# A row maximum on one core: GpSimd takes 128-column parts of rows in place of full rows, the last two rows come in chained halves, and loads are written ahead

## The chip, the cores and the metric

One core of a Trainium2 chip. The metric is the device time of one execution in microseconds (us), the slowest core's; with one core there is just that one. Most executions of a kernel agree within 0.2%.

## The reference

```python
x: float32 [32, 512, 1024]          # standard normal draws, 67.1 MB
def reference(x):
    return np.max(x, axis=-1).astype(np.float32)     # [32, 512]
```

That is 16384 rows of 1024 numbers. They are laid on 128 partitions, 128 rows on each. In this document "a row" is one such step: 1024 columns on all 128 partitions, 0.524 MB.

## The kernel before

VectorE takes the maximum of nearly all rows directly from a ring of 46 rows in SBUF. Five rows are taken from it: TensorE transposes the row (`turn`), ScalarE copies it out of PSUM, GpSimd takes the maximum over the partitions, and TensorE transposes one partition of the result back (`back`) into a small PSUM tile, which the traces call `fetched`; below this last step is the *fetch*. A tiny reduction of VectorE, the merge, ends it. The last row comes in two halves, and the result of the first half is stored in the column just ahead of the second, so that the second reduction (513 columns) takes it in. Loads are counted from 0, and step j is the stretch of the program that reduces load j.

```python
BLOCKS = [[15, 15, 15, 13, 13, 11, 9, 9, 6, 6],      # rows in each load
          [3, 3, 2, 1, 1, 1, 1, 1, 1, 1]]
RING = 46
TENSOR = {8: [("turn", 8, 0), ("back", 8, 0)],  # what TensorE does, by the step ahead of which it is written
          9: [("turn", 9, 0), ("turn", 9, 1), ("turn", 9, 2), ("back", 9, 0)],
          12: [("turn", 12, 0), ("back", 9, 1), ("back", 9, 2), ("back", 12, 0)]}
BY_GPSIMD = {8: 1, 9: 3, 12: 1}                 # load: full rows
MERGE = {9: 8, 15: 9, 18: 12}                   # after step: merge of load
...
        for n in loads:
            ...
            nc.sync.dma_start(out=xc, in_=xb[:, b:b + n, :])
            ...
            m = BY_GPSIMD.get(j, 0)
            ...
            for what, i, k in TENSOR.get(j, []):
                (turn if what == "turn" else back)(i, k)
            reduce = in_turn("DVE", nc.vector.reduce_max(
                out=cols[:, :n - m], in_=xc[:, :n - m, :], axis=X))
            if j in MERGE:
                i = MERGE[j]
                in_turn("DVE", nc.vector.reduce_max(out=tiles[i][1], in_=backs[i], axis=X))
...
    nc.sync.dma_start(out=half, in_=xb[:, b, :H])
    nc.sync.dma_start(out=tail[:, PAD:], in_=xb[:, b, H:])
    in_turn("DVE", nc.vector.reduce_max(out=tail[:, PAD - 1:PAD], in_=half, axis=X))
    in_turn("DVE", nc.vector.reduce_max(out=res[:, I - 1:], in_=tail[:, PAD - 1:], axis=X))
```

`in_turn` keeps the instructions of an engine in the order in which the program writes them. The waits between engines are not written by hand: they are derived from which instructions touch the same memory.

## Time and profile before

| | before |
|---|---|
| time, median of 3 runs | 164.49 us (164.41 to 164.53) |
| span of the profiled run | 162.6 us |
| load queue, share of 16 DMA engines | 96.6% |
| VectorE busy | 135.0 us (83%), of which 0.5 us in merges |
| GpSimd busy | 16.3 us, five maxima of 3.2 us |
| end of VectorE's last reduction | 160.36 us |

The load queue is the bound: by the packet records the DMA engines are full from 1.7 us to about 158.4 us. VectorE's reductions wait 24.3 us, all of it for loads. This line is of the waits of the kernel before (who waited for whom; us in total, times, longest). In the profile DVE is VectorE, PE TensorE, ACT ScalarE, POOL GpSimd and SP the engine that issues the loads; L139 is line 139 of that run's kernel:

```profile
DVE res L139 <- DMA ring<-in_x_dram: 24.3, 4, 18.9
```

There is no line in which a reduction of VectorE waits for TensorE.

### The profile page before, as it was taken

How to read it: one execution, taken by the hardware profiler on the slowest of the kernel's cores; microseconds unless marked ns; L12 is line 12 of the kernel's file. 1: busy time of each engine (PE TensorE's matmuls, PEld its weight loads, DVE VectorE, ACT ScalarE, POOL GpSimd, SP SyncE). 2: the span in 40 equal slices, each digit the busy share in tenths (PEclk: the TensorE clock that was granted, in tenths of full speed). 3: DMA queues.
4: the chain of work that ended last, by engine and by line, in shares of the span. 5: the costliest groups of instructions: out<-in, count | busy, mean ns of one | idle time of the engine just before them, and what ended most of it. 6: DMA issues, size and time to landing. Idle time of an engine off the chain costs nothing.

```text
span 162.6 us, 293 instructions
## 1 busy us (share of the span) xinstructions
PE 13.0 (8%) x80; PEld 11.7 (7%) x80; DVE 135.0 (83%) x33; ACT 6.3 (4%) x6; POOL 16.3 (10%) x9
## 2 busy tenths in 40 slices
PE   0000000000000000000000000000000040943520
PEld 0000000000000000000000000000000030933420
DVE  3000079995999779999996999999999999999994
ACT  3000000000000000000000000000000011240200
POOL 0000000000000000000000000000000007099910
PEclk9999999999999999999999999999999999985555
DMA  7999699988999799999998989999999999999990
GB/s 242 484 484 438 287 484 484 484 378 348 484 484 484 333 498 432 445 419 419 419 419 387 499 388 427 417 426 408 417 435 435 471 399 426 423 418 409 406 368 16
DMA packets 3456, 67.18 MB, mean 413 GB/s; under 512 B 640, under 2 KB 640, under 8 KB 1792
## 3 DMA queue, kind: packets, MB, share of 16 engines
q1 hardware_dynamic: 3168, 67.11, 96.6%
q10 hardware_dynamic: 288, 0.07, 0.2%
HBM read 67.11 MB, written 0.07 MB: 413 GB/s over the span
## 4 chain that ended last, share of the span: by engine, by line
DVE 54%; DMA 44%; SPq 0%; issue 0%
DVE res L139 53%; DMA ring<-in_x_dram 44%; DVE res L156 0%; DVE tail L155 0%; SPq L133 0%; DVE res L143 0%
## 5 line engine op out<-in xcount | busy, mean ns | idle before, releaser
L139 DVE TENSOR_REDUCE res<-ring 128x1 f32<-128x1024 f32 (+6 forms) x20 | 132.1, 6653 | 24.3 <-DMA ring<-in_x_dram 24.3
L106 POOL PARTITION_ALL_REDUCE top<-sb x5 | 16.1, 3255 | 138.8 <-ACT sb L104 138.8
L98 PE MATMUL ps<-ident,ring 128*128 128x128 f32 x40 | 8.1, 382 | 134.2 <-DMA ring<-in_x_dram 131.8
L98 PEld LDWEIGHTS ps<-ident,ring 128*128 128x128 f32 x40 | 7.1, 204 | 134.3 <-issue 134.2
L104 ACT COPY sb<-ps 128x1024 f32<-128x1024 f32 x5 | 5.1, 1013 | 144.9 <-PE ps L98 143.0
L115 PE MATMUL fetched<-ident,top 1*128 1x1 f32 x40 | 5.0, 243 | 9.1 <-POOL top L106 9.1
L115 PEld LDWEIGHTS fetched<-ident,top 1*128 1x128 f32 x40 | 4.6, 214 | 10.3 <-POOL top L106 9.8
L104 ACT ACT_TABLE_LOAD x1 | 1.3, 1283 | 0.7 <-PEq L176 0.7
L76 DVE MEMSET ident<- 128x128 f32 x1 | 0.2, 165 | 0.8 <-PEq L176 0.8
L156 DVE TENSOR_REDUCE res<-tail 128x1 f32<-128x513 f32 x1 | 0.7, 686 | 0.0
L155 DVE TENSOR_REDUCE tail<-ring 128x1 f32<-128x512 f32 x1 | 0.7, 675 | 0.0
L83 DVE TENSOR_SCALAR rowno<-rowno 32x1 f32<-32x1 f32 x3 | 0.4, 147 | 0.1
L143 DVE TENSOR_REDUCE res<-fetched 128x1 f32<-128x8 f32 (+1 forms) x3 | 0.5, 161 | 0.0
L78 DVE TENSOR_TENSOR_SCAN colno<-ident 128x128 f32<-128x128 f32 x1 | 0.4, 425 | 0.0
L85 DVE TENSOR_SCALAR ident<-colno,rowno 128x128 f32<-128x128 f32 x1 | 0.3, 287 | 0.0
L80 DVE STREAM_TRANSPOSE rowno<-colno 128x32 f32<-128x32 f32 x1 | 0.2, 211 | 0.0
L176 POOL MEMSET const-float32-0.0<- 128x1 f32 x1 | 0.1, 99 | 0.2 <-issue 0.2
L176 POOL MEMSET const-uint8-127<- 128x1 uint8 x1 | 0.1, 103 | 0.0
L176 POOL MEMSET const-bfloat16-1.0<- 128x1 bf16 x1 | 0.1, 102 | 0.0
L176 POOL MEMSET const-float32-1.0<- 128x1 f32 x1 | 0.1, 99 | 0.0
L77 DVE MEMSET rowno<- 128x32 f32 x1 | 0.1, 85 | 0.0
## 6 DMA issues: line engine op xcount, KB each, us to landing
ring<-in_x_dram SPq DMA_DIRECT2D x3, 7680.0 KB, 38.4
ring<-in_x_dram SPq DMA_DIRECT2D x2, 6656.0 KB, 34.6
ring<-in_x_dram SPq DMA_DIRECT2D x2, 4608.0 KB, 37.8
ring<-in_x_dram SPq DMA_DIRECT2D x2, 3072.0 KB, 31.9
ring<-in_x_dram SPq DMA_DIRECT2D x1, 5632.0 KB, 28.6
ring<-in_x_dram SPq DMA_DIRECT2D x7, 512.0 KB, 22.3
ring<-in_x_dram SPq DMA_DIRECT2D x2, 1536.0 KB, 34.9
ring<-in_x_dram SPq DMA_DIRECT2D x1, 1024.0 KB, 33.4
```

Source lines behind the costliest of these rows:

```text
L78: in_turn("DVE", nc.vector.tensor_tensor_scan(out=colno, data0=ident, data1=ident, initial=-1.0, op0=ALU.add, op1=ALU.mult))
L83: in_turn("DVE", nc.vector.tensor_scalar(out=part, in0=part, scalar1=float(q * 32), scalar2=None, op0=ALU.add))
L85: in_turn("DVE", nc.vector.tensor_scalar(out=ident, in0=colno, scalar1=rowno[:, 0:1], scalar2=None, op0=ALU.is_equal))
L98: in_turn("PE", nc.tensor.transpose(out=ps[:, c * P:(c + 1) * P], in_=rows[:, k, c * P:(c + 1) * P], identity=ident,))
L104: nc.scalar.copy(out=sb, in_=ps)
L106: nc.gpsimd.partition_all_reduce(top, sb, P, bass_isa.ReduceOp.max)
L115: in_turn("PE", nc.tensor.transpose(out=backs[j][:, k, c:c + 1], in_=tops[j, k][0:1, c * P:(c + 1) * P], identity=ident[0:1, 0:1],))
L139: reduce = in_turn("DVE", nc.vector.reduce_max(out=cols[:, :n - m], in_=xc[:, :n - m, :], axis=X))
L143: in_turn("DVE", nc.vector.reduce_max(out=tiles[i][1], in_=backs[i], axis=X))
L155: in_turn("DVE", nc.vector.reduce_max(out=tail[:, PAD - 1:PAD], in_=half, axis=X))
L156: in_turn("DVE", nc.vector.reduce_max(out=res[:, I - 1:], in_=tail[:, PAD - 1:], axis=X))
L176: nc = _bacc.Bacc("TRN2", target_bir_lowering=False, num_devices=1)
```

## The change

The intent, as the code shows it: VectorE and GpSimd share single rows. GpSimd takes the first 2 or 4 of a row's eight parts of 128 columns, so its chunks can be smaller and shared rows can come later, up to the third last row. VectorE takes the remaining columns of that row, its *part*. Loads are written into the program up to two steps ahead, so that TensorE's work, now one list, can be written as early as wanted. The last two rows come as two halves each. There are 22 transfers, as before.

```diff
 BLOCKS = [
-    [15, 15, 15, 13, 13, 11, 9, 9, 6, 6],
-    [3, 3, 2, 1, 1, 1, 1, 1, 1, 1],
+    [15, 15, 15, 8, 12, 11, 9, 8, 7, 7, 5],
+    [4, 3, 2, 2, 1, 1, 1],
 ]
 ...
+# load: (rows shared, parts of 128 columns that GpSimd takes of each)
+SHARED = {9: (5, 2), 11: (4, 2), 12: (2, 4), 14: (1, 2), 15: (1, 4), 17: (1, 2)}
+TENSOR = [
+    ("turn", 9, 0), ("turn", 9, 1), ("back", 9, 0), ("back", 9, 1),
+    ("turn", 11, 0), ("turn", 12, 0), ("back", 11, 0), ("turn", 14, 0),
+    ("turn", 15, 0), ("back", 12, 0), ("back", 14, 0), ("turn", 17, 0),
+    ("back", 15, 0), ("back", 17, 0),
+]
+MERGE = {10: (9,), 13: (11,), 16: (12,), 17: (14,), 20: (15, 17)}
 ...
+    def share(j):                 # PSUM: GpSimd's maxima and, in the last column, VectorE's
+        m, parts = SHARED[j]
+        if j not in backs:
+            fetched = psmall.tile([P, m, parts + (parts < C)], F32)
+            backs[j] = fetched
+        return backs[j]
 ...
+    for j in range(len(loads)):
+        while issued < len(loads) and issued < j + 3:
+            ...                   # stops where a ring place is still to be read
+            nc.sync.dma_start(out=rows(issued), in_=src)
+            issued += 1
+        while todo and (todo[0][0] == "back" or todo[0][1] < issued):
+            what, i, c = todo.pop(0)
+            (turn if what == "turn" else back)(i, c)
+        ...
+        if n > m:
+            maximum(res[:, col:col + n - m], rows(j)[:, :n - m, :])
+        if m and parts < C:
+            maximum(share(j)[:, :, parts], rows(j)[:, n - m:, parts * P:])
+        merge(j)
 ...
+    for t in range(2):            # the last two rows, two chained halves each
+        ...
```

More of the change, by code (lines that the diff above doesn't have):

```diff
@@ L13 @@
 BLOCKS = [
-    [15, 15, 15, 13, 13, 11, 9, 9, 6, 6],
-    [3, 3, 2, 1, 1, 1, 1, 1, 1, 1],
+    [15, 15, 15, 8, 12, 11, 9, 8, 7, 7, 5],
+    [4, 3, 2, 2, 1, 1, 1],
 ]
 RING = 46
-TENSOR = {
-    8: [("turn", 8, 0), ("back", 8, 0)],
-    9: [("turn", 9, 0), ("turn", 9, 1), ("turn", 9, 2), ("back", 9, 0)],
-    12: [("turn", 12, 0), ("back", 9, 1), ("back", 9, 2), ("back", 12, 0)],
-}
-BY_GPSIMD = {8: 1, 9: 3, 12: 1}
-MERGE = {9: 8, 15: 9, 18: 12}
+SHARED = {9: (5, 2), 11: (4, 2), 12: (2, 4), 14: (1, 2), 15: (1, 4), 17: (1, 2)}
[6 more added lines that the diff above has]
+MERGE = {10: (9,), 13: (11,), 16: (12,), 17: (14,), 20: (15, 17)}
 NOSYNC = mybir.DependencyInfo(mybir.DependencyClass.NoSync, mybir.DependencyReason.DATA)
@@ L53 @@
     allr = ctx.enter_context(tc.tile_pool(name="allr", bufs=2))
-    psum = ctx.enter_context(tc.tile_pool(name="psum", bufs=3, space=bass.MemoryType.PSUM))
-    psmall = ctx.enter_context(tc.tile_pool(name="psmall", bufs=2, space=bass.MemoryType.PSUM))
+    psum = ctx.enter_context(tc.tile_pool(name="psum", bufs=2, space=bass.MemoryType.PSUM))
+    psmall = ctx.enter_context(tc.tile_pool(name="psmall", bufs=4, space=bass.MemoryType.PSUM))
     ring = once.tile([P, RING, D], F32)
@@ L59 @@
     PAD = 16
-    tail = once.tile([P, PAD + H], F32)
+    tails = once.tile([P, 2, PAD + H], F32)
     latest = {}
@@ L86 @@
         out=ident, in0=colno, scalar1=rowno[:, 0:1], scalar2=None, op0=ALU.is_equal))
-    tiles = {}
-    tops = {}
-    backs = {}
-    def turn(j, k):
-        rows, cols = tiles[j]
-        ps = psum.tile([P, D], F32)
-        for c in range(C):
-            in_turn("PE", nc.tensor.transpose(
-                out=ps[:, c * P:(c + 1) * P],
-                in_=rows[:, k, c * P:(c + 1) * P],
-                identity=ident,
-            ))
-        sb = turned.tile([P, D], F32)
-        nc.scalar.copy(out=sb, in_=ps)
-        top = allr.tile([P, D], F32)
-        nc.gpsimd.partition_all_reduce(top, sb, P, bass_isa.ReduceOp.max)
-        tops[j, k] = top
-    def back(j, k):
-        if j not in backs:
-            fetched = psmall.tile([P, BY_GPSIMD[j], C], F32)
-            backs[j] = fetched
-        for c in range(C):
-            in_turn("PE", nc.tensor.transpose(
-                out=backs[j][:, k, c:c + 1],
-                in_=tops[j, k][0:1, c * P:(c + 1) * P],
-                identity=ident[0:1, 0:1],
-            ))
-    at = first = j = 0
+    loads = []
+    first = at = 0
     views = []
-    for loads in BLOCKS:
-        S = sum(loads) + (loads is BLOCKS[-1])
+    for sizes in BLOCKS:
+        S = sum(sizes) + 2 * (sizes is BLOCKS[-1])
         xb = xf[first * P:(first + S) * P, :].rearrange("(p i) d -> p i d", p=P)
@@ L128 @@
         b = 0
-        for n in loads:
+        for n in sizes:
             if at + n > RING:
                 at = 0
-            xc = ring[:, at:at + n, :]
-            nc.sync.dma_start(out=xc, in_=xb[:, b:b + n, :])
-            cols = res[:, first + b:first + b + n]
-            m = BY_GPSIMD.get(j, 0)
-            tiles[j] = xc[:, n - m:, :], cols[:, n - m:]
-            for what, i, k in TENSOR.get(j, []):
-                (turn if what == "turn" else back)(i, k)
-            reduce = in_turn("DVE", nc.vector.reduce_max(
-                out=cols[:, :n - m], in_=xc[:, :n - m, :], axis=X))
-            if j in MERGE:
-                i = MERGE[j]
-                in_turn("DVE", nc.vector.reduce_max(out=tiles[i][1], in_=backs[i], axis=X))
+            loads.append((at, n, xb[:, b:b + n, :], first + b))
@@ L144, with chunks @@
             at += n
             b += n
-            j += 1
         first += S
     assert first == I
-    if at + 1 > RING:
-        at = 0
-    half = ring[:, at, :H]
-    nc.sync.dma_start(out=half, in_=xb[:, b, :H])
-    nc.sync.dma_start(out=tail[:, PAD:], in_=xb[:, b, H:])
-    in_turn("DVE", nc.vector.reduce_max(out=tail[:, PAD - 1:PAD], in_=half, axis=X))
-    in_turn("DVE", nc.vector.reduce_max(out=res[:, I - 1:], in_=tail[:, PAD - 1:], axis=X))
+    def chunks(j):
+        m, parts = SHARED[j]
+        per = max(1, C // parts)
+        return [(r, min(per, m - r)) for r in range(0, m, per)]
@@ new lines, in rows, with turn @@
+    def rows(j):
+        start, n, _, _ = loads[j]
+        return ring[:, start:start + n, :]
+    tops = {}
+    backs = {}
+    def turn(j, c):
+        m, parts = SHARED[j]
+        r, q = chunks(j)[c]
+        W = q * parts * P
+        ps = psum.tile([P, D], F32)
+        for i in range(q):
+            for c0 in range(parts):
+                k = i * parts + c0
+                in_turn("PE", nc.tensor.transpose(
+                    out=ps[:, k * P:(k + 1) * P],
+                    in_=rows(j)[:, loads[j][1] - m + r + i, c0 * P:(c0 + 1) * P],
+                    identity=ident,
+                ))
+        sb = turned.tile([P, D], F32)
+        in_turn("ACT", nc.scalar.copy(out=sb[:, :W], in_=ps[:, :W]))
+        top = allr.tile([P, D], F32)
+        in_turn("POOL", nc.gpsimd.partition_all_reduce(
+            top[:, :W], sb[:, :W], P, bass_isa.ReduceOp.max))
+        tops[j, c] = top
@@ new lines, in share, with back @@
+    def share(j):
+        m, parts = SHARED[j]
+        if j not in backs:
+            fetched = psmall.tile([P, m, parts + (parts < C)], F32)
+            backs[j] = fetched
+        return backs[j]
+    def back(j, c):
+        m, parts = SHARED[j]
+        r, q = chunks(j)[c]
+        for i in range(q):
+            for c0 in range(parts):
+                k = i * parts + c0
+                in_turn("PE", nc.tensor.transpose(
+                    out=share(j)[:, r + i, c0:c0 + 1],
+                    in_=tops[j, c][0:1, k * P:(k + 1) * P],
+                    identity=ident[0:1, 0:1],
+                ))
@@ new lines, in maximum, with merge @@
+    def maximum(out, in_):
+        return in_turn("DVE", nc.vector.reduce_max(out=out, in_=in_, axis=X))
+    def merge(j):
+        for i in MERGE.get(j, ()):
+            _, k, _, c0 = loads[i]
+            q, _ = SHARED[i]
+            maximum(res[:, c0 + k - q:c0 + k], share(i))
+    issued = done = 0
+    todo = list(TENSOR)
+    for j in range(len(loads)):
+        while issued < len(loads) and issued < j + 3:
+            start, n, src, _ = loads[issued]
+            held = any(s < start + n and start < s + k for s, k, _, _ in loads[j:issued])
+            if held:
+                break
+            nc.sync.dma_start(out=rows(issued), in_=src)
[3 more added lines that the diff above has]
+            (turn if what == "turn" else back)(i, c)
+        _, n, _, col = loads[j]
+        m, parts = SHARED.get(j, (0, 0))
+        if n > m:
[3 more added lines that the diff above has]
+        merge(j)
@@ new lines @@
+    assert not todo
+    for t in range(2):
+        if at + 1 > RING:
+            at = 0
+        row = S - 2 + t
+        half = ring[:, at, :H]
+        at += 1
+        nc.sync.dma_start(out=half, in_=xb[:, row, :H])
+        nc.sync.dma_start(out=tails[:, t, PAD:], in_=xb[:, row, H:])
+        maximum(tails[:, t, PAD - 1:PAD], half)
+        merge(len(loads) + 2 * t)
+        last = maximum(res[:, I - 2 + t:I - 1 + t], tails[:, t, PAD - 1:])
+        merge(len(loads) + 2 * t + 1)
+        if t == 0:
+            latest_row = last
@@ L159 @@
     store = nc.scalar.dma_start(out=views[0][0], in_=views[0][1])
-    tc.add_manual_dep(store.ins, reduce.ins.name, SYNC, reason="behind the loads")
+    tc.add_manual_dep(store.ins, latest_row.ins.name, SYNC, reason="behind the loads")
     nc.scalar.dma_start(out=views[1][0], in_=views[1][1])
```

## The prediction

> **What bounds the kernel now.** I read the page first, then the timeline of VectorE, then the timeline of the last 33 us. The page, its DMA queues and the chain that ended last:
>
> ```profile
> span 162.6 us, 293 instructions
> ...
> q1 hardware_dynamic: 3168, 67.11, 96.6%
> ...
> DVE 54%; DMA 44%; SPq 0%; issue 0%
> ```
>
> The chain gives VectorE 54%, but that does not make VectorE the bound. The load queue's packets take 96.6% of the time of the 16 DMA engines, and in the trace's packet records I find no stretch from 1.7 us to 158.4 us in which the engines run dry. The timeline of VectorE agrees:
>
> ```profile
> 21.46 16.15 DVE L139 TENSOR_REDUCE res<-ring 128x15 f32<-128x15360 f32 x1 [18.95 <-DMA ring<-in_x_dram]
> 39.60 16.15 DVE L139 TENSOR_REDUCE res<-ring 128x15 f32<-128x15360 f32 x1 [1.99 <-DMA ring<-in_x_dram]
> 57.75 30.08 DVE L139 TENSOR_REDUCE res<-ring 128x15 f32<-128x15360 f32 x2 [1.99 <-DMA ring<-in_x_dram]
> 89.22 53.79 DVE L139 TENSOR_REDUCE res<-ring 128x13 f32<-128x13312 f32 x6 [1.40 <-DMA ring<-in_x_dram]
> ...
> 157.83 1.22 DVE L139 TENSOR_REDUCE res<-ring 128x1 f32<-128x1024 f32 x1
> 158.97 0.68 DVE L155 TENSOR_REDUCE tail<-ring 128x1 f32<-128x512 f32 x1
> 159.67 0.69 DVE L156 TENSOR_REDUCE res<-tail 128x1 f32<-128x513 f32 x1
> ```
>
> A load of 15 rows (a "row" is 1024 columns on 128 partitions, 0.524 MB) lands every 18.14 us, so 1.21 us a row or 434 GB/s, while VectorE needs 16.15 us for it. All 128 rows take DMA about 155 us. VectorE's own work follows a line: 16.15 us for 15360 elements and 1.21 us for 1024 give 1/0.96 ns per element plus 0.145 us, and successive reductions start some 0.08 us before the previous one ends, so about 0.065 us above the elements each. GpSimd's five full rows only save VectorE from falling behind, because 1.21 against 1.13 us leaves little room once loads are small. By the trace's landing records the last half row lands at 159.10; VectorE ends at 160.36, the store lands at 161.81 and the span is 162.6. So **at most about 0.6 us is to be had at the end**: the half before the last waits 0.5 us for VectorE (landed 158.48, started 158.97).
>
> The helpers' path, from the timeline of the last part:
>
> ```profile
> 131.75 1.94 PE L98 MATMUL ps<-ident,ring 128*128 128x128 f32 x8 [131.75 <-DMA ring<-in_x_dram]
> 133.73 1.01 ACT L104 COPY sb<-ps 128x1024 f32<-128x1024 f32 x1 [131.73 <-PE ps L98]
> 134.84 3.23 POOL L106 PARTITION_ALL_REDUCE top<-sb  x1 [134.41 <-ACT sb L104]
> ...
> 138.11 1.01 PE L115 MATMUL fetched<-ident,top 1*128 1x1 f32 x8 [4.42 <-POOL top L106]
> ```
>
> From landing (131.66) to the last fetched column (139.12) one chunk of 1024 columns takes **7.46 us**. Today VectorE reads the fetched columns only much later, in a small merge of 0.15 us, so it never waits for this path.
>
> **What the Trainium skill says.** (1) "DMA: Bandwidth & Descriptors", Specifications, gives a ceiling of 435 GB/s for the fabric; the trace's 434 GB/s agrees, so loads cannot get faster. (2) "SBUF — State Buffer", Who interferes with whom: DMA has ports of its own, and tensor_reduce on this chip never contends with GpSimd. The trace agrees: the rate was 425 GB/s with VectorE fully busy (120 to 130 us) and 416 GB/s with GpSimd, TensorE and VectorE all working (140 to 150 us; that stretch has smaller loads), and the three-row reduction beside GpSimd at 143 us took the same 3.34 us as at 139.66, before it. (3) "PSUM — Partial Sum Buffer", PSUM bank collisions raise a hardware error: two engines must not touch the same bank and 32-partition quadrant at once, whether or not the bytes overlap, so such accesses have to be ordered by a semaphore. No access in the trace of before tests this (VectorE only reads the fetched tiles after TensorE has long finished them). It decides my prediction.
>
> **The change, part by part.**
>
> *Loads.* Before 20 loads and 2 half rows, after 18 loads and 4 half rows: 22 transfers both, 67.11 MB both. The queue's time is unchanged. Each load's ring place comes free early enough: for example the 7 rows that replace rows of the third block need VectorE's reduction of the 12- and 11-row loads, done at about 107.2, and DMA reaches them near 124. So the last half again lands at about 159.1. Gain or loss 0.
>
> *Columns moved.* GpSimd had 5 rows; now it has 10+8+8+2+4+2 = 34 parts of 128 columns, 4.25 rows. VectorE gets 0.75 row more (0.8 us) and, counted in the program, 31 reductions in place of 25 (6 x 0.065 = 0.4 us), spread over the last 27 us.
>
> *The new wait.* For a shared load VectorE now writes its own part's maximum into column `parts` of the same PSUM tile into which TensorE transposes back GpSimd's result. That is one bank, all quadrants, two engines, so the two must be ordered, and I take the order to be that of the program text. The list of TensorE's work is emptied as soon as its next "turn" has its load written, and a "back" at its head is written at once. With loads written up to two ahead, the backs of load 9 are written at step 7, those of 11 at step 10, of 14 at 13, of 15 and 17 at 15: all **before** VectorE's part of that load. Only load 12 is the other way round (part at 12, back at 13). So for five of six shared loads VectorE's part of the row must wait for the whole helpers' path, and being in order, everything behind it waits too.
>
> *Load 9* (7 rows, 5 shared, 2 parts each). After 112 rows the landing is at 138.96 in both kernels; less five rows (6.1 us) load 9 lands at about 132.9. Its two full rows end at 135.2. Its GpSimd work comes in chunks of 8 parts and of 2. First chunk as above: fetched at 132.9 + 7.46 = 140.3. The second's reduction follows the first on GpSimd; a quarter of the width at proportional cost is 0.8 us, with a fixed part up to 1.5 (estimate). It is fetched at about 140.9. **VectorE idles about 5.7 us** (135.2 to 140.9).
> Then: 5 x 768 elements 4.07, load 10 (five rows) 5.40, merge 0.08: 150.5.
>
> *Load 11* (4 rows, all shared) lands at 138.96 + 4.95 = 143.9; fetched at 143.9 + 7.46 = 151.4. VectorE waits another 0.9 us and starts at 151.45.
>
> *The rest* is VectorE back to back, since every landing (last 159.1) is now behind it: 3072, 1024, 1024, 2048, 1024, 768, 512, 1024, 768, 512, 513, 512 and 513 elements = 13314 or 13.87 us, plus 13 x 0.065, five merges of 0.08 and about 0.2 for the chained halves: 15.35 us. The later waits (14, 15, 17) should be covered, because TensorE's back of 12 waits for VectorE at about 157.1, and the backs of 14, 15 and 17 follow by 158.5, 160.9 and 161.9, while VectorE needs them at 160.4, 161.3 and 163.1.
> VectorE ends at 151.45 + 15.35 = 166.8 instead of 160.36: **+6.4 to 6.5 us**. Stores behind it are as before. 164.49 + 6.5 = **171.0 us**, 4% slower.
>
> *The chained halves* alone would have gained: the 0.5 us backlog at the end shrinks by 0.2 to 0.5 us. With VectorE 7 us late this is lost.
>
> **Rivals.** (a) *No wait, or the wait on TensorE's side*: if the order is by bytes, or if the back waits for VectorE's part, VectorE never idles. I ran the same sums: it meets the landings from 152 us on, ends at about 160.2 and the kernel takes 164.3 us (164.0 to 165.2 with a dear narrow GpSimd reduction, since the last merge sits just before the last half). For it: the merges are placed as if results came late, which has a sense only if VectorE runs ahead of them. Against it: the skill's rule on banks, and the text order. I give it 13 to 15%. (b) *GpSimd has a large fixed cost*: the profile has only the 1024-wide reduction (3.23 us). If the narrow ones cost nearly as much, the second chunk of load 9 comes 2 us later, and those of 15 and 17 become waits: about 173 us. The three back to back (9.64 us, so 3.2 each) say nothing on width. (c) *Loads held up* by VectorE's lateness: against it, every ring place needed after 132 us is freed by reductions done by 117 us; worth 0. A late VectorE alone costs no transfer.
>
> **Range and chances.** Given the wait, 171.0 with about 1.5 us either way: the start of load 9's part and load 11's wait back each other up (without the second it would be 170.0). The range is 168.8 to 173.2. Slower than 167.8 (2%) happens when the wait is there: 0.84. Without it the time is within 2%: 0.14. Faster by 2% (under 161.2) would need less than DMA's time: 0.02.
>
> **What would show it.** Right: VectorE's groups show idle time before the partial reductions ended by TensorE's fetched columns, some 6 us in two or more waits, the longest just before 141 us; VectorE busy time about 136 us; the DMA line full until 158 us and then nothing while VectorE works on to 166 us. Wrong: VectorE idle only for DMA after 132 us, a last reduction at about 160 us (rival a), or narrow GpSimd reductions over 2 us (rival b).

## The result, and the profile after

| | before | after |
|---|---|---|
| median of 6 runs each, same chip | 164.44 us | **170.77 us** (170.62 to 170.90) |
| ratio | | 1.0385 (1.0372 to 1.0399) |
| VectorE busy | 135.0 us | 136.2 us |
| load queue's share | 96.6% | 93.0% of a longer span, the same work |
| end of VectorE | 160.36 us | 166.57 us |

A ratio is the mean time of one kernel's runs over that of the other's of the same rounds, so it is not quite the ratio of the medians that are quoted. The change made the kernel 3.85% slower.

The page of the changed kernel, the lines that answer to those of before:

```profile
span 168.8 us, 290 instructions
...
q1 hardware_dynamic: 3168, 67.11, 93.0%
...
DVE 46%; DMA 44%; POOL 2%; PE 2%; issue 1%; another core or an unknown queue 1%; SPq 1%; ACT 1%; DVEq 0%; ACTq 0%
```

The queue moved the same 67.11 MB in as many packets. The chain now has pieces of GpSimd (POOL) and TensorE (PE) in it that were not there before: a helper's path sets the end. By the trace's list of that chain these pieces are the path of load 11: transposes at 143.89 us, ScalarE, GpSimd at 147.03, and the fetch, which ends at 151.33. The waits of the changed kernel say who was held:

```profile
DVE res L164 <- DMA ring<-in_x_dram: 22.7, 3, 18.8
...
DVE fetched L164 <- PE fetched L157: 6.7, 2, 5.6
```

The second line is new. VectorE, about to write its part into the fetched tile, waited twice for TensorE, 6.7 us in all. The timeline of VectorE shows where (start, duration; in brackets the idle time ahead of it and its releaser):

```profile
140.65 4.16 DVE L164 TENSOR_REDUCE fetched<-ring 128x5 f32<-128x3840 f32 x1 [5.59 <-PE fetched L157]
...
144.72 5.48 DVE L164 TENSOR_REDUCE res<-ring 128x5 f32<-128x5120 f32 x1
...
151.36 3.36 DVE L164 TENSOR_REDUCE fetched<-ring 128x4 f32<-128x3072 f32 x1 [1.08 <-PE fetched L157]
...
154.62 1.21 DVE L164 TENSOR_REDUCE res<-ring 128x1 f32<-128x1024 f32 x1
...
165.90 0.68 DVE L164 TENSOR_REDUCE res<-tails 128x1 f32<-128x513 f32 x1
```

The 5 x 768 columns of load 9 lie in SBUF since 132.75 us, yet VectorE starts on them at 140.65. From 151.36 on it never idles, and it ends at 166.57, 7.7 us after the last half row has landed (158.89 in the trace). TensorE and GpSimd in the same stretch show what it waited for:

```profile
135.92 4.27 POOL L139 PARTITION_ALL_REDUCE top<-sb  x2 [135.49 <-ACT sb L137]
...
139.20 1.42 PE L157 MATMUL fetched<-ident,top 1*128 1x1 f32 x10 [3.99 <-POOL top L139]
...
147.03 3.22 POOL L139 PARTITION_ALL_REDUCE top<-sb  x1 [6.84 <-ACT sb L137]
...
150.31 1.01 PE L157 MATMUL fetched<-ident,top 1*128 1x1 f32 x8 [0.83 <-POOL top L139]
...
157.12 1.20 PE L157 MATMUL fetched<-ident,top 1*128 1x1 f32 x10 [2.20 <-DVE fetched L164]
```

TensorE's fetches of load 9 end at 140.62 and VectorE starts at 140.65; those of load 11 end at 151.32 and VectorE starts at 151.36. In both cases it reads other data and writes another column than TensorE. The last line is the control that the change itself holds: for load 12 the part is written ahead of the fetch, and there it is TensorE that waits for VectorE (2.20 us), which costs VectorE nothing.

The TensorE clock granted in the profiled runs differs: 0.947 before, 1.000 after. It does not explain the slowdown, since the slower kernel had the higher clock; and in the run with full rows for GpSimd below, executions at 0.93 and at 1.00 took the same 165.0 to 165.1 us.

### The profile page after: what moved, and what is told of

Read it like the earlier page. It is cut to its first block, busy times and chain, and to the rows that moved or that the text cites. A ratio compares the mean times of both kernels' runs of the same rounds, so it can differ in the third digit from the quotient of the medians.

```text
span 168.8 us, 290 instructions
## 1 busy us (share of the span) xinstructions
PE 13.1 (8%) x68; PEld 10.5 (6%) x68; DVE 136.2 (81%) x39; ACT 5.9 (4%) x8; POOL 14.8 (9%) x11
## 3 DMA queue, kind: packets, MB, share of 16 engines
q1 hardware_dynamic: 3168, 67.11, 93.0%
HBM read 67.11 MB, written 0.07 MB: 398 GB/s over the span
## 4 chain that ended last, share of the span: by engine, by line
DVE 46%; DMA 44%; POOL 2%; PE 2%; issue 1%; another core or an unknown queue 1%; SPq 1%; ACT 1%; DVEq 0%; ACTq 0%
DMA ring<-in_x_dram 44%; DVE res L164 42%; DVE fetched L164 4%; POOL top L139 2%; PE ps L131 1%; DVE tails L164 1%; SPq L181 1%; PE fetched L157 1%; ACT sb L137 1%; DVEq L239 0%; ACTq L137 0%
## 5 line engine op out<-in xcount | busy, mean ns | idle before, releaser
L164 DVE TENSOR_REDUCE res<-ring 128x15 f32<-128x15360 f32 (+8 forms) x15 | 121.2, 8112 | 22.7 <-DMA ring<-in_x_dram 22.7
L139 POOL PARTITION_ALL_REDUCE top<-sb x7 | 14.6, 2124 | 146.1 <-ACT sb L137 142.8
L131 PE MATMUL ps<-ident,ring 128*128 128x128 f32 x34 | 8.7, 426 | 139.7 <-DVE res L164 132.8
L164 DVE TENSOR_REDUCE fetched<-ring 128x1 f32<-128x768 f32 (+4 forms) x6 | 11.2, 1888 | 6.7 <-PE fetched L157 6.7
L131 PEld LDWEIGHTS ps<-ident,ring 128*128 128x128 f32 x34 | 6.4, 220 | 140.5 <-DVE res L164 132.8
L137 ACT COPY sb<-ps 128x1024 f32<-128x1024 f32 (+2 forms) x7 | 4.6, 678 | 152.8 <-PE ps L131 151.4
L157 PE MATMUL fetched<-ident,top 1*128 1x1 f32 x34 | 4.5, 243 | 8.7 <-POOL top L139 6.5
L164 DVE TENSOR_REDUCE res<-tails 128x1 f32<-128x513 f32 x2 | 1.4, 683 | 0.0
L164 DVE TENSOR_REDUCE tails<-ring 128x1 f32<-128x512 f32 x2 | 1.4, 676 | 0.0
L164 DVE TENSOR_REDUCE res<-fetched 128x1 f32<-128x3 f32 (+4 forms) x6 | 0.9, 156 | 0.0
```

What stands on the lines that cost most here:

```text
L131: in_turn("PE", nc.tensor.transpose(out=ps[:, k * P:(k + 1) * P], in_=rows(j)[:, loads[j][1] - m + r + i, c0 * P:(c0 + 1) * P], identity=i ...
L137: in_turn("ACT", nc.scalar.copy(out=sb[:, :W], in_=ps[:, :W]))
L139: in_turn("POOL", nc.gpsimd.partition_all_reduce(top[:, :W], sb[:, :W], P, bass_isa.ReduceOp.max))
L157: in_turn("PE", nc.tensor.transpose(out=share(j)[:, r + i, c0:c0 + 1], in_=tops[j, c][0:1, k * P:(k + 1) * P], identity=ident[0:1, 0:1],))
L164: return in_turn("DVE", nc.vector.reduce_max(out=out, in_=in_, axis=X))
```

## The experiments

The theory: VectorE's part and TensorE's fetch write one PSUM tile, so they are ordered; the order is that of the program; in five of six shared loads the fetch is written first; so VectorE waits for the whole path over ScalarE and GpSimd. Rivals: narrow parts or more instructions are slow in themselves; loads and fetches written ahead stall VectorE whatever memory is written; each wait costs its own length; the halves matter by themselves.

All runs below gave the right result. "Before" on the chip of the first four was 164.29 us, of the second four 164.36 us (9 runs each).

### Every part written ahead of the fetch

```diff
-        while todo and (todo[0][0] == "back" or todo[0][1] < issued):
+        while todo and (todo[0][1] < issued if todo[0][0] == "turn"
+                        else todo[0][1] not in PART_FIRST or todo[0][1] < j):
 ...
-    assert not todo
+    for what, i, c in todo:
+        (turn if what == "turn" else back)(i, c)
 ...
+PART_FIRST = {9, 11, 12, 14, 15, 17}
```

> The changed kernel with one thing turned round: for every shared load TensorE's fetch of GpSimd's maxima is written in the program after VectorE's own part of that load; order on each engine, loads, widths and merges stay. Theory (the wait in program order costs the time): VectorE loses both waits for the fetched columns, does its part of load 9 from about 135.0 us and not 140.65, ends at about 160.0 us in place of 166.6, and the kernel takes 164.2 us (163.9 to 164.6), 4% under the changed kernel and just under the kernel before (164.44). TensorE now waits for VectorE instead. Rival (narrow parts, more reductions or smaller loads are what is slow, whatever the order): still 168 us or more. Rival (same bank costs time whichever engine comes first, because TensorE then waits and GpSimd's later chunks slip): 165.5 to 168 us, with VectorE idle before the last merges.

Measured: **164.27 us** (164.18 to 164.39, 5 runs), ratio to before 1.0000 (0.9987 to 1.0012). The timeline of VectorE in this kernel:

```profile
135.00 4.15 DVE L166 TENSOR_REDUCE fetched<-ring 128x5 f32<-128x3840 f32 x1
139.06 5.48 DVE L166 TENSOR_REDUCE res<-ring 128x5 f32<-128x5120 f32 x1
...
144.53 3.35 DVE L166 TENSOR_REDUCE fetched<-ring 128x4 f32<-128x3072 f32 x1
...
159.42 0.69 DVE L166 TENSOR_REDUCE res<-tails 128x1 f32<-128x513 f32 x1
```

The parts start at 135.00 and 144.53 with no idle time, and the end is 160.11. Each engine executes as many instructions on the same data; only the fetches of five loads are written later (load 12's was already). The whole 6.5 us are gone, and both rivals (168 us or more; 165.5 to 168 us) with them. TensorE has no line of waiting for VectorE in this run either: GpSimd's result comes later than VectorE's part anyway.

### The part in memory of its own, program order kept

```diff
+    own = once.tile([P, 16, 2], F32)           # SBUF; owned[j] is a slice of it
 ...
-            fetched = psmall.tile([P, m, parts + (parts < C)], F32)
+            fetched = psmall.tile([P, m, parts], F32)
 ...
-            maximum(share(j)[:, :, parts], rows(j)[:, n - m:, parts * P:])
+            maximum(owned[j][:, :, 0], rows(j)[:, n - m:, parts * P:])
 ...
-            maximum(res[:, c0 + k - q:c0 + k], share(i))
+            maximum(owned[i][:, :, 1], share(i))
+            maximum(res[:, c0 + k - q:c0 + k], owned[i])
```

> The changed kernel with its program order kept (fetches still written before VectorE's part), but VectorE writes its part to a small SBUF tile, so that TensorE and VectorE no longer write one PSUM bank; each merge becomes two small reductions. Theory (the shared bank forces the wait): no wait of VectorE for TensorE before the parts, six more small reductions of some 0.08 us each, some of them beside waits for loads, end of VectorE near 160.2 us, kernel 164.4 us (164.0 to 164.9). Rival (writing fetches and loads ahead itself is what stalls VectorE, whatever memory the part goes to): 170 to 171 us, with the same 5.6 us idle.

Measured: **165.01 us** (164.94 to 165.14, 5 runs), ratio to before 1.0044 (1.0032 to 1.0057). The fetches are still written ahead of the parts, and the waits are gone, so it is the common tile that orders the two. The time is 0.1 us over the expected range, and 0.7 us over that of the first experiment. VectorE's timeline at the end shows where most of this comes from:

```profile
159.29 0.68 DVE L169 TENSOR_REDUCE tails<-ring 128x1 f32<-128x512 f32 x1
159.88 0.15 DVE L169 TENSOR_REDUCE own<-fetched 128x1 f32<-128x4 f32 x1
160.06 0.15 DVE L169 TENSOR_REDUCE res<-own 128x1 f32<-128x2 f32 x1
160.14 0.15 DVE L169 TENSOR_REDUCE own<-fetched 128x1 f32<-128x2 f32 x1
160.32 0.15 DVE L169 TENSOR_REDUCE res<-own 128x1 f32<-128x2 f32 x1
160.39 0.68 DVE L169 TENSOR_REDUCE res<-tails 128x1 f32<-128x513 f32 x1
```

I had put a further small reduction at 0.08 us, the distance of two that do not depend on one another (160.06 to 160.14). One that reads what the one in front wrote starts 0.18 us after that one started (159.88 to 160.06). So a merge of two steps takes 0.26 us. (In the two profiled runs VectorE ends 0.97 us apart; 0.18 us of that is there before any merge, at load 9's part: 135.18 us against 135.00.)

### Only the longer wait taken away (load 9)

```diff
+PART_FIRST = {9}
```

> Only load 9 turned round as in the first experiment: the longer wait (5.59 us) goes. Theory (the two waits back each other up, the last one sets the end): VectorE reaches its part of load 11 at about 144.6 us and then idles until the fetch of load 11 at 151.3, so one wait of about 6.7 us takes the place of 5.6 and 1.1; the time stays at 170.7 us (170.4 to 171.1). Rival (each wait costs its own length): 165.2 us.

Measured: **170.69 us** (170.64 to 170.84, 4 runs), against 170.77 of the changed kernel. VectorE's timeline:

```profile
135.03 4.15 DVE L166 TENSOR_REDUCE fetched<-ring 128x5 f32<-128x3840 f32 x1
...
151.40 3.36 DVE L166 TENSOR_REDUCE fetched<-ring 128x4 f32<-128x3072 f32 x1 [6.75 <-PE fetched L159]
```

A wait of 5.59 us is taken away and the time does not move. The 1.08 us in front of load 11 become 6.75, because that part starts when load 11's fetch is done, at 151.4, whenever VectorE gets there. The longest wait of the profile was worth nothing by itself.

### Only the shorter wait taken away (load 11)

```diff
+PART_FIRST = {11}
```

> Only load 11 turned round: the shorter wait (1.08 us) goes. Theory: load 9's part still starts at 140.65, VectorE then works back to back from there, the kernel gains the whole 1.1 us: 169.7 us (169.4 to 170.1), with no new wait before the parts of loads 14, 15 and 17. Rival (the waits of the later loads take its place): 170.4 us or more.

Measured: **169.55 us** (169.45 to 169.65, 4 runs), 1.2 us under the changed kernel. The two were not timed in the same rounds; by their ratios to before (1.0320 and 1.0385) it is 1.1 us. VectorE's timeline:

```profile
140.64 4.16 DVE L166 TENSOR_REDUCE fetched<-ring 128x5 f32<-128x3840 f32 x1 [5.59 <-PE fetched L159]
...
150.19 3.35 DVE L166 TENSOR_REDUCE fetched<-ring 128x4 f32<-128x3072 f32 x1
```

The whole wait of 1.08 us is gained: load 11's part starts at 150.19 and not at 151.36. The one wait left is load 9's (5.59 us).

### Both taken away, the fetches of 14, 15 and 17 left ahead

```diff
+PART_FIRST = {9, 11}
```

> Loads 9 and 11 turned round together, the fetches of 14, 15 and 17 left ahead of VectorE's parts. Theory: both waits seen in the changed kernel go, and VectorE, some 6.7 us earlier, now meets the waits of loads 14 and 15 that its lateness hid: about 2.3 us before the part of 14 and 1.4 us before that of 15. Kernel 167.8 us (167.2 to 168.4), so 3 of the 6.5 us are gained. Rival (the two waits seen are all that there is): 164.2 to 164.5 us.

Measured: **168.10 us** (167.96 to 168.19, 4 runs), ratio to before 1.0228. VectorE's timeline:

```profile
152.49 1.22 DVE L166 TENSOR_REDUCE res<-ring 128x1 f32<-128x1024 f32 x1
156.15 0.96 DVE L166 TENSOR_REDUCE fetched<-ring 128x1 f32<-128x768 f32 x1 [2.44 <-PE fetched L159]
158.53 0.69 DVE L166 TENSOR_REDUCE fetched<-ring 128x1 f32<-128x512 f32 x1 [1.42 <-PE fetched L159]
```

Two waits appear, in front of the parts of loads 14 and 15, that the changed kernel's profile does not have. They were there as dependences and did not show, because VectorE came too late to meet them.

### Loads not written ahead

```diff
-        while issued < len(loads) and issued < j + 3:
+        while issued < len(loads) and issued < j + 1:
```

> The changed kernel with loads written only at their own step, not up to two ahead; the list of TensorE's work is unchanged. By the program's order the fetches of 11, 14 and 15 then come after VectorE's parts, those of 9 and 17 stay before. Theory: the wait before load 11's part goes, that of load 9 (5.6 us) stays, a new one before load 17's part comes (1.4 us), as TensorE's fetches now wait for VectorE and GpSimd's last chunks slip to 162.7: 171.0 us (170.4 to 171.4), with VectorE's waits at loads 9 and 17. Rival (writing loads ahead is what brings the wait): near 164.4 us.

Measured: **171.03 us** (170.93 to 171.09, 4 runs), ratio to before 1.0406. The waits in it, VectorE's for TensorE and TensorE's for VectorE:

```profile
PE fetched L157 <- DVE fetched L164: 7.3, 2, 4.2
DVE fetched L164 <- PE fetched L157: 7.0, 2, 5.6
```

VectorE's two waits lie in front of load 9's part (5.59 us) and load 17's (1.40). Writing loads ahead is thus not the cause. It only decides for which loads a fetch comes ahead of the part; load 9's is ahead in both forms.

### Full rows for GpSimd, all else of the change kept

```diff
-SHARED = {9: (5, 2), 11: (4, 2), 12: (2, 4), 14: (1, 2), 15: (1, 4), 17: (1, 2)}
+SHARED = {9: (2, 8), 11: (1, 8), 12: (1, 8)}     # with TENSOR and MERGE to match
```

> The changed kernel's loads, loads written ahead and chained halves, but GpSimd takes full rows again (two of load 9, one of 11, one of 12: four in all), so VectorE writes nothing into the fetched tiles. Fetches are written far ahead as in the changed kernel. Theory: no wait for TensorE anywhere; VectorE behind by about 0.8 us at the end because it lacks the help in the last loads: ends near 160.8, kernel 164.8 us (164.5 to 165.2). Rival (fetches written ahead stall VectorE even without a shared write): 168 us or more.

Measured: **165.09 us** (165.02 to 165.13, 5 runs), ratio to before 1.0044 (1.0031 to 1.0056). VectorE writes nothing into a fetched tile and waits for no fetch, though fetches are written as far ahead as in the changed kernel. It ends at 161.03. The trace fits the expected reason, that it lacks help in the last loads: up to 152.59 us it still waits for loads, but the first of the four halves lands at 157.09 and is taken only at 158.32. No run changes this alone, so the reason is argued.

### The two chained rows alone, on the kernel before

```diff
-    [3, 3, 2, 1, 1, 1, 1, 1, 1, 1],
+    [3, 3, 2, 1, 1, 1, 1, 1, 1],
 ...                                  # the last two rows in halves, as in the change
```

> The kernel before with one part of the change alone: the last two rows, not one, come in two chained halves; GpSimd still has its five full rows. Theory: VectorE's end hardly moves, as one more reduction eats what the earlier start gives: between 0.2 us faster and 0.2 us slower than before (164.1 to 164.5 us). Rival (the halves are a gain of their own): 0.4 us or more faster.

Measured: **164.51 us** (164.44 to 164.62, 5 runs), ratio to before 1.0011 (0.9998 to 1.0023): no difference that can be told from none, and no gain.

## Why the prediction was right

- **The sum.** Predicted 171.0 us, measured 170.77. VectorE's end was put at 166.8 and is 166.57.
- **The wait and its direction.** The step on which all hung was that a common PSUM tile forces an order and that the program's order decides who waits. The first two experiments show both halves: turning the order round, or parting the memory, removes the waits. This agrees with the rule of the Trainium skill, "PSUM — Partial Sum Buffer", PSUM bank collisions raise a hardware error, by which disjoint columns of a bank are no excuse. That the chip itself would have failed without the wait is not shown by any run here: all kernels were ordered. Nor do the runs tell whether the order is derived for the bank or for the tile, since the trace does not show where the tiles lie. Another tile of the same pool is free of it: in the changed kernel VectorE starts load 14's part with no wait while TensorE is fetching load 15's columns into their own tile:

```profile
160.11 0.58 PE L157 MATMUL fetched<-ident,top 1*128 1x1 f32 x4 [1.18 <-POOL top L139]
160.27 1.54 DVE L164 TENSOR_REDUCE fetched<-ring 128x1 f32<-128x768 f32 x2
```

- **Its length.** 5.7 us were predicted in front of load 9, 5.59 came; 0.9 in front of load 11, 1.08 came. The estimate for the narrow GpSimd maximum (0.8 to 1.5 us for 256 columns) holds 1.14 us. So the rival with a large fixed cost falls: the seven maxima took about 3.22 us for 1024 columns, 1.78 for 512 and 1.14 for 256.
- **Two waits that back each other up.** This was said with "without the second it would be 170.0". Without the first the time stayed (170.69), without the second it was 169.55. The size was 0.45 us off: 0.23 is the start (171.0 against 170.77), the rest a gain of 1.1 to 1.2 us where 1.0 was said.
- **Later waits covered.** The waits of loads 14, 15 and 17 were predicted to be hidden, and were; without the first two, those of 14 and 15 showed at once (2.44 and 1.42 us; 168.10 us in all). Load 17's did not show there.
- **The rival without a wait** was given 164.3 us; with the order turned round the kernel takes 164.27.
- **The loads.** The last half was put at 159.1 us and landed at 158.89 in the trace of after. VectorE's lateness held up no transfer: the load queue's work is the same, and its packets end at 158.5 us.
- **What did not hold.** The prediction said that the chained halves alone would gain 0.2 to 0.5 us, as the backlog of 0.5 us at the end shrinks. On the kernel before they gained nothing (164.51 us against 164.36), and the backlog stayed: in that run the half before the last landed at 158.53 us and was taken at 159.06, 0.53 us later, against 0.49 before. The forecast for the whole change did not rest on it.

What the change wanted is small even where it works: with the wait gone it ties with the kernel before (1.0000). The bound is DMA, and by the prediction's estimate at most 0.6 us lay behind it. I found no version that beats the kernel before: the best of the eight is the one with the order turned round, and it equals it.

## What to carry to other kernels

Two engines that wrote different columns of one PSUM tile were ordered here all the same, in the order of the program. So write the one that is ready first ahead in the program (164.27 us here), or give each its own memory (165.01 us here, with one more small reduction in each merge). A wait's length in the profile is not its worth: ask which wait ends last (here 5.59 us were worth nothing and 1.08 us were worth 1.2), and which dependences are only hidden by the present one. And before helping an engine that is not the bound, work out how much can be had between the bound's end and the kernel's end; here it was at most about 0.6 us.

## What the Trainium skill lacked or had wrong

- "PSUM — Partial Sum Buffer", PSUM bank collisions raise a hardware error: it gives the rule but neither the cost of the waits nor that their direction is the writer's choice. Here the same guard cost 6.5 us of 164 in one direction (170.77 us) and nothing in the other (164.27 us).
- "GPSIMD Engine Reference", Cross-partition — where GPSIMD wins: its one figure for a reduction along partitions is 247,699 ns for tensor_reduce at [128, 2048]. The partition all-reduce that this kernel uses is not there; the runs show 3.22, 1.78 and 1.14 us for 1024, 512 and 256 columns on 128 partitions.
- No page that I read has a figure for a chain of tiny dependent reductions on VectorE. The runs show 0.08 us from start to start for two independent ones and 0.18 us where the second reads the first's output.
